# A two-layer hybrid decoder trunk on one core: first output projection on the right side of memory, last feed-forward sums in a region of their own, and another timing model for the order

## The chip, the cores and the metric

The kernel runs on one core of a Trainium2 chip. The metric is device time in microseconds; three runs of the kernel before gave 2640.45, 2644.82 and 2648.73, so the median is 2644.82 us.

## What is computed

The reference is a trunk of two layers over 1024 positions of width 1024, all in f32. Cut to what matters:

```python
for l in range(DEPTH):                                    # DEPTH = 2
    mod = cond @ w_mod[l] + b_mod[l]                      # 6 vectors of 1024
    sh1, sc1, gt1, sh2, sc2, gt2 = jnp.split(mod, 6)
    h = rms_norm(x, norm_g[l, 0]) * (1.0 + sc1) + sh1
    y = mixer_block(h, ...)     # h @ w_in, four mixers, group norms, @ w_o
    x = x + gt1 * rms_norm(y, norm_g[l, 1])
    h = rms_norm(x, norm_g[l, 2]) * (1.0 + sc2) + sh2
    y = jnp.square(jax.nn.relu(h @ w_up[l])) @ w_down[l]  # width 4096 inside
    x = x + gt2 * rms_norm(y, norm_g[l, 3])
```

The four mixers are a short gated convolution, sparse attention (compressed, selected and window branch, each a softmax), gated linear attention in chunks of 64, and a chunked gMLP.

## The kernel before

Activations stand with features on the 128 partitions, and 512 positions (one half, `hf`) are done at a time, so there are four rounds of mixer and feed-forward: `mix(0,0)`, `mix(0,1)`, `ff(0,0)`, `mix(1,0)`, `ff(0,1)`, `mix(1,1)`, `ff(1,0)`, `ff(1,1)`, written in that order in the code.

Each product is made of three matmuls (`mm3`, L173 to L175): weights and activations are split into a rounded high part and a rest, and high*high, high*low and low*high are summed in PSUM. So each weight tile of 128x512 that a DMA of 256 KB brings (`raw_a`, `raw_b` or `raw_f`, by lane) is cast by ACT (`A.copy(hi, raw)`, L167) and subtracted by DVE (`sub(lo, raw, hi)`, L131) before its twelve matmuls. The raw tiles have 3 buffers on lanes a and b, 5 on lane f.

The order of work on each engine is not written out by hand: the framework lists all instructions, simulates them with a timing model, and gives each engine a fixed queue, first come by priority. `tc.block(schedule_with_timeline_sim=True)` (L40 of the kernel) picks the model. Each engine then works strictly down its own queue on the chip. `LATER` (800 instructions) lowers the priority of the residual and norm after three of the four output projections.

What the steps of the change touch:

- `mods_start` and `load_x`: 16 rows of `w_mod` (`mw`, 512 KB each, 6 buffers) are multiplied with the condition on DVE (L239), and give the first scale and shift; `load_x(1)` brings the second half of x into the 8 tiles `y` that held the first half, so each of its loads waits until `make_h` has read the old tile.
- `mods_now(0, (2, 3, 4), "b")`: 48 tiles of `w_mod` through the 3 buffers `raw_b`, multiplied on DVE (L247), needed for the residual and norm that follow the first output projection. `mods_steps`: the other rows of `w_mod`, one step behind each `up` and behind every second `down` unit of `ff(0,0)` and `ff(0,1)`.
- The output projection (`gemm(p, "a", w_o[l, o], outs, ...)` in `mix`), its evacuations `yo` (L912), the sum of squares (`rms_R`, one matmul against ones at L195), `residual` (eight times L140 and L137, with `xo` loaded back from memory and the sum stored) and `make_h` (`nt`, `h`), which gives the feed-forward's input.
- `ff_body`: `up(n)` squares the ReLU (`r`, one buffer, then `hid`), `down(g)` adds eight units into the tiles `y` (L137), `finish` makes the residual of the feed-forward, with `xo` in the buffers of `hid`.
- Attention (`nsa_part`): scores (L786, L788) go to PSUM, DVE takes the maximum (L793, L799), ACT the exponential, DVE and ACT the scaling; `attend` transposes on PE (L741), splits into high and rest on ACT (L743) and DVE (L131), and multiplies with the values (L746, L747). Units of the feed-forward stand between these on PE's queue wherever the order puts them.

Of the kernel before, what the change touches and what calls it, by code (L numbers as in the profile page):

```python
# [7 lines left out]
F32 = mybir.dt.float32  # L8
# [8 lines left out]
DEPTH = 2  # L17
T = 512
# [17 lines left out]
def trunk_kernel(ctx, tc, xT, c, pos, freq, sel, w_in, conv_w, cmp_pos, cmp_w1, cmp_w2,  # L36
# [3 lines left out]
    ctx.enter_context(tc.block(schedule_with_timeline_sim=True))  # L40
# [253 lines left out]
    def mods_steps(todo):  # L294

        for l, j in todo:
            for k in range(8):
                mod_half(l, j, k, lambda src, shape: wraw("f", src, shape))
                if k == 7:
                    mod_scale(l, j, slice(0, 8))  # L300
                yield
# [574 lines left out]
    def mix(l, hf, h, between=None):  # L876
        d = par[l]
        gain = d["gain"]
        with ExitStack() as es:
            gr = es.enter_context(region("gates"))  # L880
            if l == 0 and hf == 0:
# [11 lines left out]
                lane_pool["f"] = pool("ff", side="right")  # L893
# [12 lines left out]
        with region("wo") as rg:  # L906
            y = []
            for o in range(8):
                p = ps("mm")
                gemm(p, "a", w_o[l, o], outs, range(8))  # L910
                yo = rg.tile([128, T], F32, name="yo", tag="yo", bufs=8)
                A.copy(yo, p)  # L912
                y.append(yo)
            if between is not None:
                res = between()
            with tc.high_priority(offset=-LATER[l, hf]):
                R = rms_R(y, 1.0 / 1024)
                residual(y, d["G1"], R,
                         lambda k: load(rg.tile([128, T], F32, name="xo", tag="xo", bufs=4),
                                        (xT[hf] if l == 0 else xb[hf])[:, k, :]), xa[l][hf])  # L920
                R = rms_R(y, 1.0 / 1024)
                h2[hf] = make_h(y, R, d["A2"], d["mod"][:, 3, :])
        return res

    def ff(l, hf, todo=()):
        if not todo:
            return ff_body(l, hf, None)
        steps = mods_steps(todo)
# [4 lines left out]
    def ff_body(l, hf, step):  # L933
# [28 lines left out]
        def down(g, cs=slice(0, T), ws=None):  # L962
            for n in range(8):
# [5 lines left out]
                if g == 0:  # L969
                    y[n] = ytile()  # L970
                    A.copy(y[n], p)
                else:
                    add(y[n][:, cs], y[n][:, cs], p)
# [11 lines left out]
        def finish(cs, R):  # L985
            residual(y, d["G2"], R,
                     (lambda k: xo[k]) if last else
                     (lambda k: load(ffp.tile([128, T], F32, name="xo", tag="hid", bufs=8), xa[l][hf][:, k, :])),
                     xb[hf] if l + 1 < DEPTH else out[hf], cs)
# [10 lines left out]
        for cs in parts:  # L1000
            down(NGRP - 1, cs, ws)
        Rs = [rms_R(y, 1.0 / 1024, cs=cs, mk=spare if last else nt) for cs in parts]
        for cs, R in zip(parts, Rs):
            finish(cs, R)
        return y
# [14 lines left out]
    xt = ff(0, 0, ((0, 5), (1, 1), (1, 0), (1, 2), (1, 4), (1, 3)))  # L1020
    h = norm(1, 0, xt)
    mix(1, 0, h)
    xt = ff(0, 1, ((1, 5),))
    h = norm(1, 1, xt)
# [90 lines left out]
```

## Time and profile before

| what | us |
|---|---|
| median of three runs | 2644.82 |
| the profiled execution, its own time | 2647.0 |
| its span, on which the shares below are taken | 2645.3 |
| PE (TensorE) busy | 2495.8 |
| DVE (VectorE) busy | 1629.1 |
| ACT (ScalarE) busy | 1308.1 |

The profile shows for each engine how long it worked, and for each wait of an engine which instruction of another engine, or which DMA, ended it. PEclk is the clock that was granted to TensorE as a share of 2.4 GHz. Matmuls overlap, so the time of one row is longer than its share of the engine's time; what one costs is read from a stretch with its count.

### The profile page before, as it was taken

The numbers are of one execution on the slowest core, as the hardware profiler recorded it, in microseconds if no ns is written. First come the engines' busy times: TensorE is split into PE (matmuls) and PEld (weight loads), VectorE is DVE, ScalarE is ACT, GpSimd is POOL, SyncE is SP. The second block draws the span as 40 slices with busy tenths as digits, with TensorE's granted clock in tenths as the row PEclk, the third lists the DMA queues.
The fourth block names the chain that finished last, engine by engine and source line by source line (L and its number), as shares of the span: only waits on it lengthen the run. The fifth ranks groups of instructions, "written<-read, shape, count | busy, mean of one in ns | idle before, by whom it ended". The sixth has DMA issues, their size and how long they took to land.

```text
span 2645.3 us, 34444 instructions
## 1 busy us (share of the span) xinstructions
PE 2495.8 (94%) x11834; PEld 1985.5 (75%) x11834; DVE 1629.1 (62%) x3425; ACT 1308.1 (49%) x2657; POOL 53.4 (2%) x65
## 2 busy tenths in 40 slices
PE   4899769999999998999999999999999999899997
PEld 2677447777788776877787877877788877688886
DVE  7576885466888468454576476544567846634445
ACT  4464444544566445444466445453466744444333
POOL 0100000000000000000100000000100000000000
PEclk9799889999999999999999999999999999999999
DMA  8212753345444346322322344222422133533332
GB/s 296 69 53 81 222 175 124 112 128 167 125 131 128 112 129 204 100 83 78 117 80 76 112 140 148 93 84 77 120 76 68 56 108 112 175 97 98 97 96 76
DMA packets 176200, 305.79 MB, mean 116 GB/s; under 512 B 21573, under 2 KB 33434, under 8 KB 176026
## 3 DMA queue, kind: packets, MB, share of 16 engines
q1 hardware_dynamic: 176026, 303.60, 37.1%
q8 instruction: 93, 1.52, 0.2%
q14 instruction: 81, 0.66, 0.1%
HBM read 281.50 MB, written 17.83 MB: 113 GB/s over the span
## 4 chain that ended last, share of the span: by engine, by line
PE 83%; DVE 8%; DMA 6%; issue 2%; ACT 1%; SPq 0%; POOL 0%; DVEq 0%; ACTq 0%; POOLq 0%
PE ps_ff L173 16%; PE ps_ff L174 16%; PE ps_ff L175 16%; PE ps_mm L173 7%; PE ps_mm L174 7%; PE ps_mm L175 7%; DMA raw_f<-in_w_mod_dram 1%; PE ps_pv L747 1%; PE ps_pv L746 1%; PE ps_mm L741 1%; DMA raw_b<-in_w_mod_dram 1%; PE ps_s L786 1%; PE ps_s L788 1%; PE ps_t L741 1%; PE ps_t L195 1%
## 5 line engine op out<-in xcount | busy, mean ns | idle before, releaser
L167 ACT CAST w_f<-raw_f 128x512 fp32r<-128x512 f32 x504 | 311.6, 619 | 462.9 <-PE ps_ff L174 432.5
L131 DVE TENSOR_TENSOR w_f<-raw_f,w_f 128x512 fp32r<-128x512 f32 x504 | 348.9, 693 | 222.8 <-ACT w_f L167 197.6
L173 PE MATMUL ps_ff<-h,w_f 128*128 128x512 f32 x1024 | 406.2, 397 | 30.8 <-ACT r L945 25.1
L175 PE MATMUL ps_ff<-h,w_f 128*128 128x512 f32 x1024 | 408.1, 399 | 0.0
L173 PE MATMUL ps_ff<-hid,w_f 128*128 128x512 f32 x992 | 394.3, 398 | 12.5 <-ACT nt L188 5.4
L174 PE MATMUL ps_ff<-h,w_f 128*128 128x512 f32 x1024 | 406.1, 397 | 0.0
L174 PE MATMUL ps_ff<-hid,w_f 128*128 128x512 f32 x992 | 391.5, 395 | 0.0
L175 PE MATMUL ps_ff<-hid,w_f 128*128 128x512 f32 x992 | 390.4, 394 | 0.0
L173 PE MATMUL ps_mm<-h,w_a 128*128 128x512 f32 x832 | 337.5, 406 | 12.6 <-ACT h L209 10.4
L175 PE MATMUL ps_mm<-h,w_a 128*128 128x512 f32 x832 | 336.7, 405 | 6.9 <-DVE w_a L131 6.7
L174 PE MATMUL ps_mm<-h,w_a 128*128 128x512 f32 x832 | 335.9, 404 | 7.4 <-DVE h L140 5.7
L167 ACT CAST w_a<-raw_a 128x512 fp32r<-128x512 f32 x208 | 128.8, 619 | 308.9 <-PE ps_mm L174 276.4
L131 DVE TENSOR_TENSOR w_a<-raw_a,w_a 128x512 fp32r<-128x512 f32 x208 | 143.1, 688 | 195.1 <-ACT w_a L167 174.9
L173 PEld LDWEIGHTS ps_ff<-h,w_f 128*128 128x128 f32 x1024 | 194.7, 190 | 77.5 <-ACT r L945 26.4
L137 DVE TENSOR_TENSOR y<-y,ps_ff 128x512 f32<-128x512 f32 (+1 forms) x232 | 154.2, 666 | 142.2 <-PE ps_ff L175 140.5
L173 PEld LDWEIGHTS ps_ff<-hid,w_f 128*128 128x128 f32 x992 | 187.0, 189 | 60.1 <-ACT nt L188 6.2
L175 PEld LDWEIGHTS ps_ff<-h,w_f 128*128 128x128 f32 x1024 | 194.6, 190 | 44.9 <-issue 4.1
L174 PEld LDWEIGHTS ps_ff<-h,w_f 128*128 128x128 f32 x1024 | 194.9, 190 | 42.7 <-issue 1.9
L175 PEld LDWEIGHTS ps_ff<-hid,w_f 128*128 128x128 f32 x992 | 186.9, 188 | 41.5 <-issue 1.9
L174 PEld LDWEIGHTS ps_ff<-hid,w_f 128*128 128x128 f32 x992 | 187.1, 189 | 41.3 <-issue 3.1
L173 PEld LDWEIGHTS ps_mm<-h,w_a 128*128 128x128 f32 x832 | 158.7, 191 | 60.2 <-ACT h L209 14.0
L174 PEld LDWEIGHTS ps_mm<-h,w_a 128*128 128x128 f32 x832 | 158.7, 191 | 50.5 <-DVE h L140 8.9
(363 smaller groups left out, 3494.5 us busy)
## 6 DMA issues: line engine op xcount, KB each, us to landing
raw_f<-in_w_up_dram SPq DMA_DIRECT2D x256, 256.0 KB, 2.8
raw_f<-in_w_down_dram SPq DMA_DIRECT2D x256, 256.0 KB, 2.6
raw_a<-in_w_in_dram SPq DMA_DIRECT2D x144, 256.0 KB, 2.7
raw_f<-in_w_mod_dram SPq DMA_DIRECT2D x112, 256.0 KB, 2.9
raw_a<-in_w_o_dram SPq DMA_DIRECT2D x64, 256.0 KB, 2.7
raw_b<-in_w_mod_dram SPq DMA_DIRECT2D x48, 256.0 KB, 3.3
mw<-in_w_mod_dram SPq DMA_DIRECT2D x16, 512.0 KB, 7.2
raw_b<-in_w_in_dram SPq DMA_DIRECT2D x32, 256.0 KB, 2.7
```

Source lines behind the costliest of these rows:

```text
L131: V.tensor_tensor(out=out, in0=a, in1=b, op=ALU.subtract)
L137: eng.tensor_tensor(out=out, in0=a, in1=b, op=ALU.add)
L167: A.copy(hi, raw)
L173: PE.matmul(ps_ap, wh, xh, start=start, stop=False)
L174: PE.matmul(ps_ap, wh, xl, start=False, stop=False)
L175: PE.matmul(ps_ap, wl, xh, start=False, stop=stop)
L195: PE.matmul(p, ones, acc, start=True, stop=True)
L741: PE.transpose(tp[0:kn, hh, :], cols(h0 + hh), ident)
L746: PE.matmul(pv[:, h0:h0 + nh, :], vst, th[0:kn], start=first[0], stop=False)
L747: PE.matmul(pv[:, h0:h0 + nh, :], vst, tl[0:kn], start=False, stop=last)
L786: PE.matmul(sp[:, 0:w], qh[:, h0 + hh, :], KX[:, 128 * k0:128 * k0 + w], start=True, stop=False)
L788: PE.matmul(sp[:, 0:w], ql[:, h0 + hh, :], KX[:, 128 * k0:128 * k0 + w], start=False, stop=True)
```

## The change

The order is now made with the framework's simpler timing model, as the line that picked the other one is gone. In the first mixer round only (`opening`), the region of the output projection stands on the right side of the on-chip memory, the eight inputs are taken in another order (attention and linear attention first), `xo` has 8 buffers in place of 4, and the feed-forward's pool is opened after that region and no longer before it. The steps of `mods_steps` begin after 5 calls in `ff(0,0)` and after 20 in `ff(0,1)`. For three of the four feed-forward rounds the last `down` group writes its sums into new tiles `yf` of a region `fin`, where also `xo` has its own 4 buffers, and the norm of the next layer is made in it; the last round, `ff(1,1)`, stays as it was.

```diff
-    ctx.enter_context(tc.block(schedule_with_timeline_sim=True))
...
-    def mods_steps(todo):
-
+    def mods_steps(todo, skip):
+
+        for _ in range(skip):
+            yield
...
-                lane_pool["f"] = pool("ff", side="right")
...
-        with region("wo") as rg:
+        opening = (l, hf) == (0, 0)
+        with region("wo", "right" if opening else "left") as rg:
...
-                gemm(p, "a", w_o[l, o], outs, range(8))
+                gemm(p, "a", w_o[l, o], outs, (6, 7, 4, 5, 2, 3, 0, 1) if opening else range(8))
...
-                         lambda k: load(rg.tile([128, T], F32, name="xo", tag="xo", bufs=4),
+                         lambda k: load(rg.tile([128, T], F32, name="xo", tag="xo", bufs=8 if opening else 4),
...
+        if opening:
+            lane_pool["f"] = pool("ff", side="right")
...
-        steps = mods_steps(todo)
+        steps = mods_steps(todo, 5 if hf == 0 else 20)
...
-                    add(y[n][:, cs], y[n][:, cs], p)
+                    yn = yo() if yo else y[n]
+                    add(yn[:, cs], y[n][:, cs], p)
+                    y[n] = yn
...
+        with region("fin") as rg:
+            down(NGRP - 1, yo=lambda: rg.tile([128, T], F32, name="yf", tag="yf", bufs=8))
+            R = rms_R(y, 1.0 / 1024)
+            finish(slice(0, T), R,
+                   lambda k: load(rg.tile([128, T], F32, name="xo", tag="xo", bufs=4), xa[l][hf][:, k, :]),
+                   xb[hf] if l + 1 < DEPTH else out[hf])
+            return norm(l + 1, hf, y) if l + 1 < DEPTH else None
```

No instruction of the computation is added or taken away; nearly all of them move. Three places show how. Lines of the kernel after are one less than before down to `mods_steps`, and one more behind the next few.

The first is the DMA queue (SP) at the program's start: `mw` are the first rows of `w_mod`, `y` the tiles of x (the first eight are the first half, the next eight the second), `raw_a` the first weights of the input projection. Before:

```order
L110 DMA conv_107<-in_conv_w_dram 128x6
L110 DMA gain_108<-in_gains_dram 128x8
L158 DMA raw_a<-in_w_in_dram 128x512 x2
L158 DMA raw_a<-in_cmp_w_dram 128x128
L265 DMA mw<-in_w_mod_dram 128x1024
L158 DMA raw_b<-in_w_in_dram 128x512 x3
L265 DMA mw<-in_w_mod_dram 128x1024 x4
L1011 DMA y<-in_xT_dram 128x512
```

And now:

```order
L264 DMA mw<-in_w_mod_dram 128x1024 x16
L109 DMA conv_97<-in_conv_w_dram 128x6
L109 DMA gain_98<-in_gains_dram 128x8
L109 DMA ng_104<-in_norm_g_dram 128x32
L109 DMA bmod_105<-in_b_mod_dram 128x48
L109 DMA conv_106<-in_conv_w_dram 128x6
L109 DMA gain_107<-in_gains_dram 128x8
L1022 DMA y<-in_xT_dram 128x512 x8
L157 DMA raw_a<-in_w_in_dram 128x512 x2
```

The first weights have moved behind all sixteen `mw` and behind the eight loads of the second half of x.

The second is DVE's queue where the residual of the output projection of `mix(0,1)` is made (`yo` with the factor `G`), while units of `ff(0,0)` run (`w_f`, `y`). Before:

```order
L137 TENSOR_TENSOR y<-y,ps_ff 128x512
L131 TENSOR_TENSOR w_f<-raw_f,w_f 128x512
L140 SCALAR_TENSOR_TENSOR yo<-yo,G_102,nt 128x512 x8
L137 TENSOR_TENSOR yo<-yo,xo 128x512
L137 TENSOR_TENSOR y<-y,ps_ff 128x512
L137 TENSOR_TENSOR yo<-yo,xo 128x512
L131 TENSOR_TENSOR w_f<-raw_f,w_f 128x512
L137 TENSOR_TENSOR yo<-yo,xo 128x512 x2
```

And now:

```order
L139 SCALAR_TENSOR_TENSOR yo<-yo,G_101,nt 128x512 x2
L130 TENSOR_TENSOR w_f<-raw_f,w_f 128x512
L136 TENSOR_TENSOR y<-y,ps_ff 128x512
L130 TENSOR_TENSOR w_f<-raw_f,w_f 128x512
L246 ISA raw_f,mp<-raw_f,cond 128x512
L246 ISA mp 128x1
L136 TENSOR_TENSOR yo<-yo,xo 128x512
L136 TENSOR_TENSOR y<-y,ps_ff 128x512
L130 TENSOR_TENSOR w_f<-raw_f,w_f 128x512
L139 SCALAR_TENSOR_TENSOR mod_108<-mp,bmod_105 128x1
L136 TENSOR_TENSOR yo<-yo,xo 128x512
L139 SCALAR_TENSOR_TENSOR yo<-yo,G_101,nt 128x512
```

The block of eight has become single instructions among those of the feed-forward, and steps of `mods_steps` (L246) have come between.

The third is PE's queue in the attention of `mix(0,1)`: `ps_s` are scores, `ps_t` and `ps_mm` from `bp` transposes, `ps_pv` the product with the values, `ps_ff` matmuls of the feed-forward. Before, where eighteen matmuls of the feed-forward follow one product of the values:

```order
L747 MATMUL ps_pv<-w_a,VS 128x512
L746 MATMUL ps_pv<-w_a,VS 128x512
L741 MATMUL ps_t<-ident,bp 128x128 x4
L173 MATMUL ps_ff<-h,w_f 128x512
L747 MATMUL ps_pv<-w_a,VS 128x512
L746 MATMUL ps_pv<-w_a,VS 128x512
L174 MATMUL ps_ff<-h,w_f 128x512
L175 MATMUL ps_ff<-h,w_f 128x512
```

And now:

```order
L172 MATMUL ps_ff<-hid,w_f 128x512
L787 MATMUL ps_s<-KW,qh 128x512
L789 MATMUL ps_s<-KW,ql 128x512
L747 MATMUL ps_pv<-w_a,VS 128x512
L808 MATMUL ps_s<-KW,qh 128x128
L809 MATMUL ps_s<-KW,ql 128x128
L808 MATMUL ps_s<-KW,qh 128x128
L748 MATMUL ps_pv<-w_a,VS 128x512
L747 MATMUL ps_pv<-w_a,VS 128x512
L742 MATMUL ps_mm<-ident,bp 128x128 x4
L809 MATMUL ps_s<-KW,ql 128x128
```

From the first score of an attention to the first matmul of its output projection there stood 729, 368 and 632 matmuls of the feed-forward in `mix(0,1)`, `mix(1,0)` and `mix(1,1)`; now there stand 267, 118 and 252. The others now follow the output projections, where the queue holds feed-forward alone for longer.

## Rows read from the trace of the kernel before

**Rows 1.** The page: span, PE and DVE in its first part, and the granted clock in forty slices.

```profile
span 2645.3 us, 34444 instructions
PE 2495.8 (94%) x11834; PEld 1985.5 (75%) x11834; DVE 1629.1 (62%) x3425; ACT 1308.1 (49%) x2657; POOL 53.4 (2%) x65
...
PEclk9799889999999999999999999999999999999999
```

**Rows 2.** Who PE waited for, over the whole span: us in total, times, longest us.

```profile
PE ps_t L195 <- DVE nt L137: 40.5, 3, 19.7
PE ps_ff L173 <- ACT r L945: 25.1, 3, 11.0
```

**Rows 3.** Busy time of each engine in stretches of 50 us: stretch and its length, PE, PEld, DVE, ACT, POOL with counts, granted clock, DMA share, GB/s.

```profile
350.00:400.00 50.00, 27.36 (x103) 20.29 (x102) 38.68 (x68) 22.07 (x36) 0.70 (x1) 0.76 0.43 141
...
950.00:1000.00 50.00, 44.12 (x183) 34.60 (x182) 41.92 (x69) 27.03 (x47) 0.00 (x0) 0.97 0.45 138
1000.00:1050.00 50.00, 40.23 (x165) 31.93 (x164) 41.13 (x84) 24.15 (x41) 0.76 (x1) 0.90 0.68 228
...
1500.00:1550.00 50.00, 44.70 (x190) 34.97 (x189) 33.73 (x54) 22.74 (x39) 0.00 (x0) 1.00 0.44 144
...
1600.00:1650.00 50.00, 45.00 (x183) 35.74 (x183) 35.86 (x56) 26.15 (x45) 0.00 (x0) 0.94 0.52 168
...
2200.00:2250.00 50.00, 46.97 (x195) 37.22 (x194) 34.96 (x55) 25.68 (x43) 0.00 (x0) 0.97 0.38 126
2250.00:2300.00 50.00, 39.00 (x163) 31.52 (x162) 36.30 (x58) 22.62 (x39) 0.00 (x0) 0.90 0.62 204
```

**Rows 4.** The same columns for the three attention stretches, from the first score to the output projection, and for 300 us of feed-forward alone.

```profile
621.50:867.40 245.90, 243.81 (x1180) 197.16 (x1178) 202.19 (x529) 152.98 (x371) 0.00 (x0) 1.00 0.43 132
1314.20:1435.70 121.50, 121.50 (x605) 98.86 (x602) 85.74 (x229) 81.89 (x213) 0.00 (x0) 1.00 0.27 78
1913.90:2133.20 219.30, 219.30 (x1084) 179.08 (x1084) 160.22 (x373) 145.49 (x353) 0.00 (x0) 1.00 0.24 69
2300.00:2600.00 300.00, 300.00 (x1325) 248.41 (x1324) 125.70 (x190) 122.21 (x205) 0.00 (x0) 1.00 0.33 100
```

**Rows 5.** DVE in order of time where `ff(1,0)` ends, and the matmul that waited: start, us, instruction, and in brackets the idle time before it and what ended it.

```profile
2280.10 5.38 DVE L140 SCALAR_TENSOR_TENSOR y<-y,G,nt 128x512 f32<-128x512 f32 x8
2285.40 1.29 DVE L137 TENSOR_TENSOR y<-y,xo 128x512 f32<-128x512 f32 x2
...
2290.82 0.68 DVE L131 TENSOR_TENSOR hid<-r,hid 128x512 fp32r<-128x512 f32 x1
...
2292.19 0.80 PE L173 MATMUL ps_ff<-h,w_f 128*128 128x512 f32 x1 [11.00 <-ACT r L945]
```

**Rows 6.** PE's instructions in order of time around 350 us (columns as in rows 5).

```profile
350.87 1.02 PE L195 MATMUL ps_t<-nt,ones 128*128 128x512 f32 x2
371.55 2.08 PE L195 MATMUL ps_t<-nt,ones 128*128 128x512 f32 x2 [19.66 <-DVE nt L137]
376.61 1.22 PE L173 MATMUL ps_ff<-h,w_f 128*128 128x512 f32 x2 [2.98 <-ACT h L209]
```

**Rows 7.** The 48 tiles of `w_mod` on lane b: the first 24 loads in the DMA queue in order of time, the last product on DVE, and the page's row of these loads (KB each, median us to landing).

```profile
254.95 34.38 SPq L158 DMA_DIRECT2D raw_b<-in_w_mod_dram  x24
...
334.50 0.68 DVE L247 CUSTOM_DVE_ANT_0 raw_b<-raw_b,cond 128x512 f32<-128x512 f32 x1
...
raw_b<-in_w_mod_dram SPq DMA_DIRECT2D x48, 256.0 KB, 3.3
```

**Rows 8.** The start: the first weights and the last load of x in the DMA queue, PE's first gemm matmul and the last of its first 48, DVE's groups of the first 54 us for lanes a and b, and stretches of 10 us (columns as in rows 3).

```profile
18.41 1.66 SPq L158 DMA_DIRECT2D raw_a<-in_w_in_dram  x2
...
49.70 0.33 SPq L1011 DMA_DIRECT2D y<-in_xT_dram  x1
...
29.40 0.80 PE L173 MATMUL ps_mm<-h,w_a 128*128 128x512 f32 x1 [0.80 <-ACT h L209]
...
52.62 0.40 PE L175 MATMUL ps_mm<-h,w_a 128*128 128x512 f32 x1
...
L131 DVE TENSOR_TENSOR w_a<-raw_a,w_a 128x512 fp32r<-128x512 f32 x5 | 3.4, 670 | 0.1
...
L131 DVE TENSOR_TENSOR w_b<-raw_b,w_b 128x512 fp32r<-128x512 f32 x2 | 1.4, 680 | 0.0
...
20.00:30.00 10.00, 4.26 (x7) 1.90 (x7) 9.56 (x20) 4.54 (x7) 0.00 (x0) 1.00 0.91 314
30.00:40.00 10.00, 3.21 (x6) 1.62 (x6) 9.81 (x21) 1.57 (x3) 0.00 (x0) 1.00 1.04 401
...
60.00:70.00 10.00, 7.99 (x28) 3.64 (x26) 2.13 (x5) 4.63 (x12) 0.00 (x0) 0.83 0.43 143
70.00:80.00 10.00, 8.87 (x26) 6.73 (x26) 5.80 (x11) 2.88 (x6) 2.56 (x2) 0.66 0.25 79
```

**Rows 9.** Groups of DVE's instructions in the whole span: count, busy us, mean ns of one, idle time before them and what ended it.

```profile
L131 DVE TENSOR_TENSOR w_f<-raw_f,w_f 128x512 fp32r<-128x512 f32 x504 | 348.9, 693 | 222.8 <-ACT w_f L167 197.6 <-PE ps_ff L175 20.1 <-PE ps_ff L174 2.6
L137 DVE TENSOR_TENSOR y<-y,ps_ff 128x512 f32<-128x512 f32 x216 | 147.6, 684 | 138.8 <-PE ps_ff L175 137.8
...
L131 DVE TENSOR_TENSOR hid<-r,hid 128x512 fp32r<-128x512 f32 x128 | 88.1, 688 | 62.4 <-ACT hid L948 62.1
...
L247 DVE CUSTOM_DVE_ANT_0 raw_f<-raw_f,cond 128x512 f32<-128x512 f32 x112 | 78.1, 699 | 65.1 <-DMA raw_f<-in_w_mod_dram 64.8
```

More of the change, by code (lines that the diff above doesn't have):

```diff
@@ L960, in wlast, with down @@
             return hi, lo
-        def down(g, cs=slice(0, T), ws=None):
+        def down(g, cs=slice(0, T), ws=None, yo=None):
             for n in range(8):
@@ L983, in ff_body, with finish @@
         xo = [load(spare(), xa[l][hf][:, k, :]) for k in range(8)] if last else None
[L985 to L989, printed above, removed]
+        def finish(cs, R, xo, o):
+            residual(y, d["G2"], R, xo, o, cs)
         for n in range(G):
@@ L999, in ff_body @@
         ws = [wlast(n) for n in range(8)] if last else None
[L1000 to L1005, printed above, removed]
+        if last:
+            for cs in parts:
+                down(NGRP - 1, cs, ws)
+            Rs = [rms_R(y, 1.0 / 1024, cs=cs, mk=spare) for cs in parts]
+            for cs, R in zip(parts, Rs):
+                finish(cs, R, lambda k: xo[k], out[hf])
+            return None
+        with region("fin") as rg:
[5 more added lines that the diff above has]
+            return norm(l + 1, hf, y) if l + 1 < DEPTH else None
     def load_x(hf):
@@ L1019, in trunk_kernel @@
     mix(0, 1, h)
-    xt = ff(0, 0, ((0, 5), (1, 1), (1, 0), (1, 2), (1, 4), (1, 3)))
-    h = norm(1, 0, xt)
+    h = ff(0, 0, ((0, 5), (1, 1), (1, 0), (1, 2), (1, 4), (1, 3)))
     mix(1, 0, h)
-    xt = ff(0, 1, ((1, 5),))
-    h = norm(1, 1, xt)
+    h = ff(0, 1, ((1, 5),))
     mix(1, 1, h)
```

## Prediction

> **What bounds the kernel now.** Read the page first: PE is busy for 2495.8 of 2645.3 us, DVE for 1629.1 [rows 1]. PE's work is the same before and after, so a change of order can only touch the 149.5 us in which PE stands idle and the stretches in which it runs at a lower clock. Then read who PE waits for: two waits hold 65.6 us, the sum of squares (L195) behind DVE's additions, 40.5 us, and the first matmul of a feed-forward unit behind ACT's `r`, 25.1 us [rows 2]. Both are the same thing, a residual and norm of some sixteen 0.6 to 0.7 us instructions that DVE does in one block while PE's queue needs something behind it. Then read where: the stretches of 50 us show it at 350, at 950 to 1050, at 1500, at 1600 and at 2200 to 2300, and in all but one of them the granted clock falls too [rows 3]. Last read what is well filled: in the three attention stretches PE is idle for 2.1 of 586.7 us, though DVE works 82%, 71% and 73% of them [rows 4]. One matmul of feed-forward alone costs 300.00 / 1325 = 0.2264 us [rows 4]; that is the unit of all that follows.
>
> The sum is made against the profiled execution's own 2647.0 us (its span of 2645.3 and 1.7 around it); the median of the three runs is 2.2 lower, and so is the forecast.
>
> **The later boundaries: -35 us.** The stretches from 950 to 1050, 1500, 1600 and 2200 to 2300 hold 5.9 + 9.8 + 5.3 + 5.0 + 3.0 + 11.0 = 40.0 us of idle PE, and their granted clocks of 0.97, 0.90, 0.94, 0.97 and 0.90 cost 1.3 + 4.0 + 2.7 + 1.4 + 3.9 = 13.3 more: 53 us [rows 3]. After an output projection the residual no longer stands as a block but between the feed-forward units, which are there in plenty because the attention used fewer; DVE has time for them, since in feed-forward alone it is busy for 125.7 of 300 us [rows 4]. I leave 2 us there. At the end of a feed-forward the block does not go. In `ff(1,0)` the subtraction `hid` for which PE waits began 10.7 us after the residual's first instruction [rows 5]. In the order of the change it stands behind 8 scalings (5.4 us), 6 additions (3.7 us) and, but for `ff(1,0)`, two sums (1.3 us), while PE has 31 matmuls (7.0 us) from where the block begins: 3.4 us of wait, and by the ratio of the 1600 stretch (2.7 of clock to 5.0 of idle) 2 us of clock. Three such ends make 16, so 18 of 53 stay. Own `xo` buffers in `fin` let these loads start without `hid`'s buffers; with 4 of them the fifth load waits for the first addition, and four further vector instructions stand before its use. I give that nothing. Bounds: -45, if the waits go wholly, and -15, if the blocks only change places.
>
> **The first output projection: -4 us.** At 350 the wait of 19.66 us ends with a sum of squares at 371.55, and the feed-forward starts at 376.61 [rows 6]; 22.6 us idle and a clock of 0.76 over 27.4 us of work make 29 us lost [rows 3]. PE's queue had this sum of squares and the feed-forward before the rest of the next mixer; now the mixer's matmuls come first, so this wait goes. But the 48 tiles of `w_mod` come earlier in DVE's queue: all of their products now stand before the weights of the fourth of eight output tiles. In the trace they took from 254.95 to 335.2, 80 us [rows 7]. In front of PE are then 31 matmuls of the convolution and 72 of the projection, 23 us. From the first of these loads to 376.61 PE did some 276 matmuls of gemms in 121.7 us. Now, at the trace's pace, 80 us and then the other 173 in 39 us make 119; at the pace that three buffers allow (3.3 us to landing, 0.69 for the product, 0.33 for the issue, through three: 1.44 us a tile [rows 7]) 69 + 39 = 108. A residual block in front of the next mixer's weights costs 10 us of DVE against 26 matmuls, 6 us: 4 more. Between -10 and +2; I take the middle. The other order of inputs lets the projection begin before the convolution's part is split; that lies behind the same DVE queue and is costed at nothing. The right side and the later pool only decide which memory the loads wait for; 8 `xo` in place of 4 end the waits inside the residual, which the mixer's matmuls now cover. Bounds for all this: -12 and +8.
>
> **The start: +5 us.** The first weights of the input projection now wait behind eight loads of x, each of which waits for DVE to have read the old tile. In the trace DVE is busy for 9.6 and 9.8 of 10 us there, the weights were issued at 18.41, the last of those eight loads at 49.70, and PE began at 29.40 and had 48 matmuls done at 53.0 [rows 8]. Without the five `w_a` and two `w_b` subtractions (4.8 us) DVE comes to that read about 46; issue, landing and cast put PE's first gemm near 50, and 48 matmuls take 10.9 us and 2 more at the lower clock: 63 instead of 53. Some 5 come back between 60 and 80, where PE lost 3.1 us of idleness and, at clocks of 0.83 and 0.66, 4.4 us [rows 8], since the rope matmuls now stand among gemms. Bounds: -3 and +12. The first attention, with its linear attention and gMLP, is mixed anew as well; no row separates it, so 0, with 10 us each way, a tenth of a hundred us, which is what the clock of 0.7 to 0.9 there leaves open [rows 1].
>
> **The three later attentions: +17 us.** With 462, 250 and 380 matmuls fewer, their stretches would be 245.9 - 104.6 = 141, 121.5 - 56.6 = 65 and 219.3 - 86.0 = 133 us of PE, 339 in all, if PE stayed as full. DVE loses 41, 19 and 30 weight subtractions, 40 products of `w_mod` (the first stretch alone), 28, 13 and 24 additions of `y`, 7, 7 and 9 of `hid`, at 693, 699, 684 and 688 ns [rows 9]: 80, 27 and 43 us, which leaves 122, 59 and 117. That is 86%, 91% and 88% of PE's time, where it was 82%, 71% and 73%. Behind a product with the values there is less on PE's queue that waits for nobody, and a score, its softmax and the split must come round through ACT and DVE. The nearest row is the stretch with 82%, which lost 1%; the far one is 950 to 1050, where PE waited on vector blocks and lost 21 of 100 us with the clock [rows 3]. I take 5%, 17 us, near the nearest; ends 0 and 68. The matmuls taken out run later at 0.2264 each, where nothing else is needed. The shift of `mods_steps` by 5 and 20 calls moves 0.7 us products into units in which DVE is half idle: nothing.
>
> The sum: -35 - 4 + 5 + 17 = -17, so 2630 against 2647.0, and **2628** against the median.
>
> The Trainium skill ("TensorE: Matmul & The Clock Gate", section "HAM oscillation — how this bites in real kernels") says that an array which falls idle between bursts, again and again, is put back to its slower clock each time, so that every burst begins slow. The trace agrees at the blocks, where idle time and a granted clock of 0.76 to 0.97 come together [rows 3]; in the attention the clock is 1.00, with PE full [rows 4].
>
> **The rivals.** *The attention starves PE (slower).* If the three stretches lose 20%, as at 950 to 1050, they cost 68 and not 17: 2679. For it: DVE at 86 to 91%, ACT close behind, and chains through three queues in fixed order. Against it: the first stretch at 82% lost 1%. It decides from a tenth on: 34 us use up the gain.
> *The clock falls there too.* Short waits that recur bring the lower clock: at 0.83, as at 60 to 70 us [rows 8], 339 us cost 70 more: 2698. For it: every idle stretch of rows 3 but one. Against it: waits under a microsecond did not do it in rows 4. This is what the skill's rule above would make of it.
> *The blocks only change places.* If half of the 35 stays, because residual and norm hold up another unit, the time is 2646, no change. For it: the end of a feed-forward still has its block. Against it: eight scalings in a row are gone after the projections.
> *The attention costs nothing.* Then 2611. For it: the 82% stretch. Against it: 91% has no precedent in this trace.
>
> **Chances.** A difference under 0.3% (8 us) cannot be told from none. Forecast 0.42, with 2612 to 2642 as its own range; attention free 0.12; blocks change places 0.16; attention starves 0.22; clock too 0.08. Faster is the forecast but a tenth, and the free attention: 0.50. Same is most of the changed places and the rest of the forecast: 0.18. Slower is 0.32. The range runs from 2595, somewhat under the free attention, to 2685, somewhat over the starved one.
>
> **What would show it.** The wait of the sum of squares behind DVE falls from 40.5 to under 15 us; the feed-forward's wait for `r` to about 10, with three ends of 3 to 4. The attention stretches last about 148, 68 and 140 us, at a clock of 1.00, with DVE over 80%. PE's first gemm starts near 50 us. In the fourth tile of the first projection PE waits 30 us or more for a weight subtraction, and none of 20 us for a sum of squares follows. I am wrong if PE is idle for more than a tenth of the attention, if the clock falls there, or if the blocks at the feed-forward's ends cost as much as before.

## The result, and the profile after

The changed kernel takes 2674.64 us (median of 4 runs, 2670.19 to 2678.22) where the kernel before takes 2643.7 on the same chip: a ratio of 1.0112, interval 1.01 to 1.0125. It is 31 us slower; 2628 had been forecast, and the time lies in the upper part of the range that went to 2685. The profiled execution of after has a span of 2668.5 us, 23.2 more than that of before [rows 1]; that is less than 31 because it is the shortest of the four (2670.19), while that of before, at 2647.0, is longer than its median. What follows accounts for the 23.

The page of after: span, busy time, and of the 40 slices the rows of PE and of its granted clock.

```profile
span 2668.5 us, 34592 instructions
...
PE 2503.8 (94%) x11834; PEld 1971.2 (74%) x11834; DVE 1635.8 (61%) x3425; ACT 1315.0 (49%) x2657; POOL 52.6 (2%) x65
...
PE   2999489999999998999999998999999999999998
...
PEclk9999699999999999999999999999999999999999
```

PE's row shows two holes, the first slice (2 tenths) and the fifth (4 tenths, with a clock of 0.6); the fifth is the first output projection. Who PE waited for (us in total, times, longest):

```profile
PE ps_mm L172 <- ACT w_a L166: 37.6, 3, 31.2
PE ps_t L194 <- DVE nt L136: 31.0, 6, 16.8
PE ps_ff L174 <- DVE w_f L130: 19.5, 3, 8.2
PE ps_mm L172 <- ACT yo L913: 16.1, 1, 16.1
```

The wait of a unit of feed-forward for ACT's `r`, 25.1 us [rows 2], is gone. In its place stands one of 19.5 us for `w_f` behind DVE, three times (8.2, 7.0 and 4.3), which no step of the prediction names. The 31.2 us of the first row are the start of the program, the first gemm. Of the 31.0 for the sum of squares, 16.8 are at the start too, where before had 16.2.

Stretches of 50 us (width, then busy us and count of PE, of the weight loads, DVE, ACT and POOL, the granted clock, DMA share, GB/s):

```profile
0.00:50.00 50.00, 2.08 (x2) 0.50 (x2) 39.44 (x88) 18.14 (x28) 1.51 (x9) 1.00 0.81 277
...
250.00:300.00 50.00, 31.19 (x119) 22.98 (x118) 37.66 (x94) 17.15 (x30) 0.00 (x0) 0.80 0.52 164
300.00:350.00 50.00, 28.06 (x102) 20.56 (x101) 39.66 (x99) 18.30 (x30) 1.16 (x1) 0.76 0.64 207
...
750.00:800.00 50.00, 47.30 (x199) 37.89 (x198) 46.11 (x95) 24.09 (x41) 0.00 (x0) 0.97 0.68 215
...
1000.00:1050.00 50.00, 42.48 (x183) 33.77 (x182) 33.31 (x53) 24.17 (x41) 0.00 (x0) 0.96 0.39 129
1050.00:1100.00 50.00, 49.23 (x197) 37.86 (x198) 32.54 (x55) 22.24 (x38) 0.64 (x1) 0.94 0.34 103
...
1650.00:1700.00 50.00, 42.87 (x173) 32.81 (x172) 39.25 (x63) 26.59 (x45) 0.81 (x1) 0.93 0.44 139
...
1850.00:1900.00 50.00, 49.80 (x255) 38.05 (x254) 41.77 (x120) 40.71 (x116) 0.00 (x0) 1.00 0.14 41
...
2300.00:2350.00 50.00, 45.72 (x192) 36.92 (x192) 23.86 (x36) 21.77 (x38) 0.00 (x0) 0.97 0.46 147
```

Beside [rows 3] and [rows 4]: the stretches that hold the end of a feed-forward (1000 to 1100, 1650, 2300) still lose idle time and clock; the one at 1850 lies in the third of the later attentions and is full. The stretch at 300 is the first output projection.

Where the 23 us came from is read at equal places in PE's queue: the same instruction of before and after, and each feed-forward matmul that stands in a stretch more or fewer counted at the 0.2264 us of [rows 4]. The times are those of the instructions in the two traces, the counts those of all of PE's matmuls between them; they differ by feed-forward matmuls alone.

| stretch | before: us, matmuls | after: us, matmuls | after minus before, counts evened out | forecast |
|---|---|---|---|---|
| start to the gMLP of mixer (0,1) | 419.3, 1558 | 412.9, 1478 | +11.7 | +1 |
| rest of mixer (0,1), to the last gemm of the attention's inputs | 185.6, 917 | 122.2, 619 | +4.1 | 0 |
| mixer (1,0) from its convolution, to the same gemm | 242.1, 1160 | 162.2, 787 | +4.5 | 0 |
| mixer (1,1), likewise | 241.5, 1158 | 162.2, 787 | +4.7 | 0 |
| three later attentions, to the output projection | 262.6, 135.8, 229.7 (1279, 767, 1173) | 152.1, 81.2, 148.1 (798, 499, 784) | -1.6, +6.1, +6.5 | +17 |
| projection (0,1) to convolution (1,0) | 190.4, 730 | 371.6, 1514 | +3.7 | in the -35 |
| projection (1,0) to convolution (1,1) | 226.2, 915 | 371.5, 1568 | -2.5 | in the -35 |
| projection (1,1) to the last feed-forward matmul | 498.8, 2174 | 671.8, 2997 | -13.3 | in the -35 |

The sum is +23.9. The attentions cost 11, the boundaries give back only 12, the opening costs 12, and the mixers 13.

In the mixers the loss is in part plain idle time. Mixer (1,0), before and then after, in the columns of the stretches above:

```profile
1057.90:1300.00 242.10, 242.10 (x1162) 191.85 (x1161) 122.81 (x224) 106.75 (x198) 9.28 (x11) 1.00 0.30 91
```

```profile
1058.80:1221.00 162.20, 159.34 (x789) 120.83 (x788) 89.92 (x175) 73.69 (x142) 10.26 (x12) 1.00 0.27 85
```

With 411 feed-forward matmuls among its own, PE never stood; with 38 it stands for 2.9 of the 4.5 us.

### The profile page after: what moved, and what is told of

Same layout as the page of the kernel before. It is cut to its first block, busy times and chain, and to the rows that moved or that the text cites. A ratio compares the mean times of both kernels' runs of the same rounds, so it can differ in the third digit from the quotient of the medians.

```text
span 2668.5 us, 34592 instructions
## 1 busy us (share of the span) xinstructions
PE 2503.8 (94%) x11834; PEld 1971.2 (74%) x11834; DVE 1635.8 (61%) x3425; ACT 1315.0 (49%) x2657; POOL 52.6 (2%) x65
## 5 line engine op out<-in xcount | busy, mean ns | idle before, releaser
L174 PE MATMUL ps_ff<-h,w_f 128*128 128x512 f32 x1024 | 405.6, 396 | 19.5 <-DVE w_f L130 19.5
L136 DVE TENSOR_TENSOR y<-y,ps_ff 128x512 f32<-128x512 f32 (+1 forms) x208 | 138.3, 665 | 173.9 <-PE ps_ff L174 172.6
```

What stands on the lines that cost most here:

```text
L136: eng.tensor_tensor(out=out, in0=a, in1=b, op=ALU.add)
L174: PE.matmul(ps_ap, wl, xh, start=False, stop=stop)
```

## The experiments

All twelve are compared with the kernel before on the same chip; its medians there lie between 2644.5 and 2647.4 us (2643.7 beside the changed kernel), so differences of a few microseconds between two of these runs say nothing. First, which part of the change costs the time.

**All edits, the old model.**

```diff
+    ctx.enter_context(tc.block(schedule_with_timeline_sim=True))
```

> The kernel after, with the old timing model put back; regions, the opening and the skipped steps stay as changed. Theory A (the model's order costs the 31 us): about 2645, within 10 of the kernel before. Theory B (the regions, the opening and the skipped steps cost them, whatever the model): 2665 to 2680. If the edits help under the old model too, it falls under 2636.

2646.28 us, ratio 0.9999 (0.999 to 1.0009): theory A.

**The model alone.** The kernel before without that line, and no other edit.

```diff
-    ctx.enter_context(tc.block(schedule_with_timeline_sim=True))
```

> The kernel before, with the one line of the timing model taken out and nothing else. Theory A: 2675 or more (more, if the other edits were made to mend this order: then 2685 to 2720). Theory B: about 2645.

2668.1 us, ratio 1.0084 (1.006 to 1.0108), between the two theories and nearer to A. So the timing model by which the order is made costs about 22 us by itself; the edits cost nothing under the old model, and under the new one some 6, which is not clear of the noise (the changed kernel's interval begins at 1.01). Counted as in the table, the trace of this run loses 2.3 us in the opening, 14.3 in the mixers and 11.8 in the attentions, and gains 8.8 at the boundaries: the losses of mixers and attentions come with the model alone, most of the opening's only where model and edits meet (the edits under the old model lose 2.9 there). That the edits as a whole are neutral does not mean that each is; two stretches of the run with all edits and the old model point to one that pays:

```profile
950.00:1000.00 50.00, 49.67 (x216) 40.19 (x216) 40.01 (x64) 28.90 (x49) 0.00 (x0) 1.00 0.53 175
1000.00:1050.00 50.00, 49.59 (x216) 40.00 (x215) 36.49 (x58) 30.35 (x51) 0.00 (x0) 1.00 0.50 160
```

The kernel before lost 5.9 and 9.8 us of idle time here, with a clock of 0.97 and 0.90 [rows 3].

**The second half's x later.**

```diff
-    xt = load_x(1)
+    with tc.high_priority(offset=-400):
+        xt = load_x(1)
```

> The kernel after, with the loads of x's second half put later in the DMA queue, behind the first weights. If the first weights' place behind these loads costs the opening its time, PE's first gemm moves from 50 to about 30 to 40 us and the time falls by 5 to 10 us against the kernel after (2665 to 2670). If the opening is held by DVE's products of w_mod anyway, under 3 us.

2672.91 us, ratio 1.0103 (1.0084 to 1.0122). PE's first gemm starts at 43.3 instead of 50.0, not at 30 to 40, and the whole gains under 2 us, less than can be told from nothing: what is won at the start is not found again at the end.

**The opening's edits undone.**

```diff
-        opening = (l, hf) == (0, 0)
+        opening = False
...
+                lane_pool["f"] = pool("ff", side="right")
```

> The kernel after, with the first output projection on the left again, inputs in the old order, 4 buffers for xo and the pool opened before it. If this part helps the new order, the time rises to 2680 to 2700. If the wait of 31 us in the projection's fourth tile comes from it, the time falls to 2650 to 2660 and that wait goes; if it comes from the 48 tiles of w_mod in front, the wait stays and the time is within 5 us of 2675.

2675.97 us, ratio 1.0118 (1.0101 to 1.0136): no difference in the whole. The wait of 31 us that the expectation puts into the projection's fourth tile is the one at the start of the program; in the projection the wait of 16.1 us for `yo` is gone, and behind it one of 16.9 for the sum of squares stands again, as in the kernel before (19.7). In its trace the gMLP of mixer (0,1) is reached at 409.7 us, with the counts evened out as early as before, so the 11.7 us of the opening are gone there; by the convolution of (1,0) it stands at +18.4, where the changed kernel has +17.9. The opening's edits move a loss of 12 us in front of that gMLP; without them it falls behind it, in the rest of mixer (0,1) (+6.3 in place of +4.1), in its attention (+3.0 in place of -1.6) and after its projection (+9.1 in place of +3.7). Why was not found.

**The modulation steps at their old place.**

```diff
-        steps = mods_steps(todo, 5 if hf == 0 else 20)
+        steps = mods_steps(todo, 0)
```

> The changed kernel with the modulation steps at the first feed-forward units again (no calls skipped). Theory A (the 4 us that ff(0,0) loses beside these steps come with the steps wherever they stand): 2675, within 4. Rival (the moved steps are what helps ff(0,0) against the kernel with the model alone, whose stretch 750 to 850 lost 13 us where the changed kernel lost 5): 2680 to 2686. Second rival (the move costs): 2668 or less.

2676.41 us, ratio 1.0131 (1.0112 to 1.0149). The skip is worth nothing in the whole that can be told here, as forecast and as theory A says.

Second, what in the new order costs it. The table says that the mixers lost their filler, the feed-forward units that stood among their matmuls, and take some 13 us longer.

**Filler back by priority, 60 and 200 steps.**

```diff
-    mix(0, 1, h)
+    with tc.high_priority(offset=-60):
+        mix(0, 1, h)
```

(and `mix(1, 0, h)`, `mix(1, 1, h)` likewise; the other run has -200.)

> The changed kernel, with the mixers of (0,1), (1,0) and (1,1) put back by 60 steps of priority, so that feed-forward units again stand among their matmuls: in PE's queue some 310 to 320 between the convolution and the last projection of the attention's inputs, and about 420 in the attention, where the changed kernel has none and 130 to 270. Theory A (what the simpler timing model costs is the missing filler: about 13 us in the three mixers and 11 in the attentions, while the gain at the boundaries stays): 2674 - 24 = 2650, range 2640 to 2658. Theory B (the new order inside the stages costs the time, on DVE, ACT or the DMA queues, and filler does not help): 2668 to 2680.

> As the run with 60 steps, with 200: 100 to 180 feed-forward matmuls more in the mixers and attentions, and 53 (12 us) of the next feed-forward between the end of one and the next convolution. Theory A (filler, and cover at the ends of the feed-forwards, where the changed kernel loses 13 + 10 us at the first two): 10 us less than with 60 steps, 2640, range 2628 to 2652; the waits of the matmul with the ones fall from 31 us to under 15. Theory B (filler does not help): 2668 to 2680. Rival C (the feed-forward's units run out before the residual after the output projection is done, as in the kernel before, and that wait comes back): 2655 to 2670, with a wait for ACT r or a sum of squares of over 10 us.

2834.86 us (ratio 1.0721, 1.0705 to 1.0737) and 2850.34 us (1.0778, 1.0762 to 1.0794). All theories missed this by over 150 us. The 60 steps also put more there than the expectation says: some 630 to 670 feed-forward matmuls more in each mixer, not 310 to 320, and 438 to 694 in the attentions, not about 420. Waits and stretches of the run with 60 steps:

```profile
PE ps_t L194 <- DVE nt L136: 82.3, 8, 17.7
...
PE ps_ff L172 <- DVE yf L136: 36.4, 3, 12.2
```

```profile
1000.00:1050.00 50.00, 25.51 (x100) 18.56 (x99) 27.62 (x42) 19.50 (x34) 0.00 (x0) 0.75 0.43 137
...
1700.00:1750.00 50.00, 20.72 (x73) 15.08 (x72) 37.02 (x56) 20.20 (x32) 0.00 (x0) 0.69 0.34 111
```

The sum of squares is waited for 82.3 us, and stretches after the projections are down to 25.51 and 20.72 us of PE at clocks of 0.75 and 0.69. At equal places in PE's queue the three stretches from an output projection to the end of the feed-forward behind it cost about 73 us more than before (changed kernel: 12 fewer), the attentions 51 (11 more), the mixers 52 (13 more). The first number is rival C of the second run, far beyond its size: a unit that is spent as filler is missing behind the projection. The others are no want of filler. In mixer (1,1) PE's queue now changes 910 times within 1447 matmuls between feed-forward and mixer, 104 times within 1158 in the kernel before. From one start to the next it takes 259 ns in the mean where a feed-forward matmul is followed by one of the mixer (242 in the kernel before), and 217 the other way (208 before), so a pair of changes takes 26 ns more, which over 455 pairs is 12 of the 18 us that this mixer loses. In this order, filler one matmul at a time costs more than none. That the changing itself is the cause is argued: no run has as much filler in larger pieces, and at the 104 changes of before other matmuls stand.

**Filler back in blocks.** The feed-forward is made a generator, and one unit of it is written behind each gemm of the gates, the linear attention and the attention's inputs.

```diff
+    def fill():
+        if unit.get(0) is not None:
+            next(unit[0])
...
         gemm(p, lane, w_in[l, GLA0], h)
+        fill()
...
-        steps = mods_steps(todo, 5 if hf == 0 else 20)
+        steps = mods_steps(todo, 14 if hf == 0 else 29)
```

(The modulation steps so begin nine calls later; what that is worth by itself was not run.)

> The changed kernel with the next feed-forward written out unit by unit behind the gemms of the gates, the linear attention and the attention's inputs, so that 178, 85 and 85 of its matmuls stand there in blocks of 12 and 24, where the changed kernel has none; in the attention nearly the same number stays. Theory A (the run with 60 steps failed because its filler came one matmul at a time and in such number that none was left for the blocks after the projections; the 4.4 us that each mixer loses beside the kernel before are for want of filler): 8 to 13 us less, 2664, range 2658 to 2669. Theory B (filler in the mixers costs as much as it covers, so its want explains nothing): 2671 to 2680. Theory C (as with 60 steps, each such matmul makes it worse): over 2685.

2667.01 us, ratio 1.008 (1.006 to 1.01). Theory A, inside its range: 7.6 us less at the median, just short of the 8 to 13, though the two intervals touch and the profiled span is only 3.2 shorter (its opening, which the edit does not touch, took 3.7 longer). In the table's terms mixers (1,0) and (1,1) lose 2.9 and 3.1 us instead of 4.5 and 4.7, with 123 feed-forward matmuls in each instead of 38; mixer (0,1) loses 4.4, no less, though it has 192 instead of 14. The idle time of mixer (1,0) is about halved:

```profile
1062.80:1242.60 179.80, 178.25 (x873) 137.05 (x874) 95.11 (x183) 82.03 (x157) 10.11 (x12) 1.00 0.28 88
```

So filler in blocks pays in two of the three mixers, a third of what its want was held to cost there, and a fifth over all three. That is little: in the traces of runs that leave these two mixers alone they lose between 3.4 and 4.7. Theory C, that any filler does harm, falls.

**The next feed-forward put forward by 300 steps.**

```diff
-    h = ff(0, 1, ((1, 5),))
+    with tc.high_priority(offset=300):
+        h = ff(0, 1, ((1, 5),))
```

(and the other two.)

> The changed kernel with the three feed-forwards ff(0,0), ff(0,1) and ff(1,0) put forward by 300 steps of priority. In PE's queue that changes little but the end of ff(0,0), where 197 matmuls of ff(0,1) instead of 72 now stand before the next convolution, and the end of ff(1,0); the mixers and attentions keep their order. Theory A (the ends of the feed-forwards cost 13, 10 and 6 us in the changed kernel because too little that waits for nobody stands behind them): 8 us come back at the first, 2 or 3 at the third: 2664, range 2658 to 2670, and the wait of the matmul with the ones falls from 31 us to under 20. Theory B (the end waits on the vector block itself, whatever stands behind it in the queue): 2671 to 2678.

2659.38 us, ratio 1.005 (1.0034 to 1.0066): about 15 us less, within theory A's range and half as much again as its 10 or 11. The sign that it named failed: the wait for the matmul with the ones is 34.9 us, not under 20. The three ends, the first in two stretches as it lies later here:

```profile
1000.00:1050.00 50.00, 49.67 (x217) 39.88 (x216) 25.06 (x39) 24.31 (x41) 0.00 (x0) 1.00 0.31 95
1050.00:1100.00 50.00, 48.19 (x205) 37.50 (x204) 39.64 (x65) 30.59 (x53) 0.85 (x1) 1.00 0.48 152
...
1650.00:1700.00 50.00, 43.09 (x172) 32.95 (x171) 35.13 (x57) 23.25 (x39) 0.64 (x1) 0.90 0.41 132
...
2300.00:2350.00 50.00, 49.70 (x219) 40.84 (x218) 17.49 (x27) 24.55 (x43) 0.00 (x0) 1.00 0.34 100
```

The first and the third are mended (42.48 at 0.96 with 49.23 at 0.94, and 45.72 at 0.97, in the changed kernel), the second is not: there PE still waits 6.8 us for `w_f`. At the third the residual has left: it is made at 2529 to 2546, in the midst of ff(1,1), and there too single weights stand among it. At the first it is what stands in DVE's queue that differs. DVE at the end of ff(0,0) in this run (start, duration):

```profile
1055.12 1.42 DVE L139 SCALAR_TENSOR_TENSOR yf<-yf,G,nt 128x512 f32<-128x512 f32 x2 [2.04 <-ACT nt L199]
1056.45 0.68 DVE L130 TENSOR_TENSOR w_f<-raw_f,w_f 128x512 fp32r<-128x512 f32 x1
1057.05 1.28 DVE L136 TENSOR_TENSOR yf<-yf,xo 128x512 f32<-128x512 f32 x2
...
1059.52 0.68 DVE L130 TENSOR_TENSOR w_f<-raw_f,w_f 128x512 fp32r<-128x512 f32 x1
```

A weight of the next feed-forward (`w_f`) comes after every two or three instructions of the residual. In the changed kernel's own trace it does not:

```profile
1034.72 0.69 DVE L130 TENSOR_TENSOR w_f<-raw_f,w_f 128x512 fp32r<-128x512 f32 x1 [2.51 <-ACT w_f L166]
1035.33 1.41 DVE L139 SCALAR_TENSOR_TENSOR yf<-yf,G,nt 128x512 f32<-128x512 f32 x2
...
1047.55 0.68 DVE L130 TENSOR_TENSOR hid<-r,hid 128x512 fp32r<-128x512 f32 x1
...
1049.35 0.68 DVE L136 TENSOR_TENSOR nt<-nt 128x512 f32<-128x512 f32 x1
1049.95 0.68 DVE L130 TENSOR_TENSOR w_f<-raw_f,w_f 128x512 fp32r<-128x512 f32 x1
```

The residual begins at 1035.33, and the weight half that PE needs is subtracted only at 1049.95, 14.6 us later. PE, in the same place:

```profile
1050.69 0.80 PE L174 MATMUL ps_ff<-h,w_f 128*128 128x512 f32 x1 [8.18 <-DVE w_f L130]
```

**Both together.**

```diff
         g, unit[0] = unit[0], None
-        return rest(g)
+        with tc.high_priority(offset=300):
+            return rest(g)
```

> The changed kernel with both: the next feed-forward written out unit by unit in the three mixers, and what is left of it put forward by 300 steps. In PE's queue 192 matmuls now stand between the end of ff(0,0) and the next convolution, and 185 at the end of ff(0,1), where the changed kernel has 72 and 72 and the run with 300 steps alone 197 and 72; the mixers keep their units. Theory A (the ends lack cover and the mixers lack filler, and there are units enough for both): the 15 us of the run with 300 steps, 4 to 8 of the run with units, and 7 more at the end of ff(0,1): 2674 - 28 = 2646, range 2640 to 2653; the stretch of 50 us that holds the end of ff(0,1) shows PE at 48 us or more. Theory B (both live on the same units, which then lack elsewhere): 2656 to 2665.

2665.97 us, ratio 1.0071 (1.0054 to 1.0088): slower than the run with 300 steps alone, as theory B says, if a microsecond beyond its range. The edit did not do what the expectation says: mixers (1,0) and (1,1) have not kept their units but hold 38 and 36 feed-forward matmuls, as in the changed kernel. The units are spent at the ends, and there the wait for `w_f` still stands, 7.5 and 4.6 us (8.2 and 7.0 in the changed kernel):

```profile
PE ps_ff L174 <- DVE w_f L130: 12.2, 2, 7.5
```

This is so although 213 feed-forward matmuls now start between the last addition into `yf` of ff(0,0) and the next convolution, where the changed kernel has 69 and the run with 300 steps 146. DVE there:

```profile
1081.96 0.69 DVE L130 TENSOR_TENSOR hid<-r,hid 128x512 fp32r<-128x512 f32 x1 [0.98 <-ACT hid L967]
1082.57 1.41 DVE L139 SCALAR_TENSOR_TENSOR yf<-yf,G,nt 128x512 f32<-128x512 f32 x2
...
1095.53 0.68 DVE L136 TENSOR_TENSOR nt<-nt 128x512 f32<-128x512 f32 x1
1096.13 0.68 DVE L130 TENSOR_TENSOR w_f<-raw_f,w_f 128x512 fp32r<-128x512 f32 x1
```

The residual comes later, at 1082.57, and is a block again: 13.6 us to the next `w_f`, and PE has by then used up its weights. Of the 213 matmuls 48 are left when the residual begins, as in the changed kernel (49); the run with 300 steps has 99 left. So more matmuls in front of the block only put the stall off. Where weights stand among the residual's instructions, it is gone, and there more matmuls are left behind the residual's start as well; as these need those weights, no run parts the two.

Last, a version that beats both kernels.

**The old model with only the region for the last sums.** Of the edits only `fin` is kept: `down` adds its last group into `yf`, and `norm` follows there.

```diff
+        with region("fin") as rg:
+            down(NGRP - 1, yo=lambda: rg.tile([128, T], F32, name="yf", tag="yf", bufs=8))
```

> The kernel before, with its timing model, and of the edits only the own region for the last feed-forward sums. By the trace of the run with all edits under the old model, the ends of ff(0,0) and ff(0,1) then lose 26 us less, the end of ff(1,0) 8 more, and what was lost there in the opening and after the moved modulation steps (17 us at 550 to 700 and 1250 to 1350) is absent here. Theory A (edits and model are separate, this one is a gain that the others hid): 2647 - 18 = 2629, range 2618 to 2640. Rival (a gain at one boundary is given back at the next, whatever else is done): 2643 to 2649.

2631.54 us, ratio 0.9952 (0.9937 to 0.9967), as theory A said in the whole. In its parts it was too large: counted as in the table, the trace gains 7 and 13 us where ff(0,0) and ff(0,1) end and loses 4 behind, where 26 less and 8 more were expected. Beside [rows 3] (40.23 at 0.90 and 45.00 at 0.94):

```profile
1000.00:1050.00 50.00, 47.38 (x204) 37.89 (x204) 42.81 (x87) 27.88 (x48) 0.00 (x0) 1.00 0.64 212
...
1600.00:1650.00 50.00, 49.58 (x215) 39.67 (x214) 36.89 (x58) 30.59 (x53) 0.00 (x0) 1.00 0.48 153
```

**The same in layer 0 alone.** ff(1,0) keeps its old end.

```diff
-        if last:
+        if l + 1 == DEPTH:
```

> As the run with the old model and the region for the last sums, but with the old end for ff(1,0), so that only ff(0,0) and ff(0,1) add into the region. In that run the end of ff(1,0) cost 17 us more than before, of which 12 came back in ff(1,1). Theory A (the region helps where a norm and a mixer follow, and costs 5 us net where only ff(1,1) follows): 2626, range 2621 to 2630. Rival (the end's place in the order moves with what precedes it, and nothing is saved): 2630 to 2636.

2633.21 us, ratio 0.9953 (0.9937 to 0.9969): the same. The end of ff(1,0) comes 14 us earlier in the trace (2245.0 against 2259.1), and nothing of it is left at the last feed-forward matmul (2617.8 against 2615.4). The rival is right.

## Why the prediction was wrong, point by point

**The start, +5: right in kind and size.** PE's first gemm starts at 50.0 us, as forecast, and up to the convolution of (0,0) the loss is 7.3 us, within -3 to +12.

**The first output projection, -4: within its bounds, by another wait.** The 48 products of `w_mod` ran from the first issue at 262.6 to 333.4, 71 us, between the 69 and 80 of the working, and the 20 us for a sum of squares [rows 6] are gone. But PE stood 4.69 us for the ones and then 16.06 not for a weight subtraction, as forecast (30 or more), but for a copy of a finished output tile by ACT. And the other order of the inputs, costed at nothing, was not free: the attention's part, now the first, was not yet split when PE came to it, and PE waited 7.97 us (3.3 in the run with the opening's edits undone). PE there:

```profile
292.23 0.79 PE L172 MATMUL ps_mm<-h,w_a 128*128 128x512 f32 x1 [7.97 <-ACT h L221]
...
312.31 2.07 PE L194 MATMUL ps_t<-nt,ones 128*128 128x512 f32 x2 [4.69 <-DVE nt L136]
330.44 0.79 PE L172 MATMUL ps_mm<-h,w_a 128*128 128x512 f32 x1 [16.06 <-ACT yo L913]
331.03 0.63 PE L173 MATMUL ps_mm<-h,w_a 128*128 128x512 f32 x1
331.46 0.63 PE L174 MATMUL ps_mm<-h,w_a 128*128 128x512 f32 x1
...
335.67 0.39 PE L172 MATMUL ps_mm<-h,w_a 128*128 128x512 f32 x1
335.90 0.39 PE L173 MATMUL ps_mm<-h,w_a 128*128 128x512 f32 x1
```

and ACT:

```profile
329.19 0.72 ACT L208 ACTIVATE h<-nt,mod 128x512 fp32r<-128x512 f32 x1 [0.62 <-DVE nt L139]
329.82 1.05 ACT L913 COPY yo<-ps_mm 128x512 f32<-128x512 f32 x2
```

The copy stood in ACT's queue behind the casts of the next norm, which wait for DVE's scalings, which stand among the products of `w_mod`. I had followed DVE's queue and PE's, not ACT's. The projection came to +4.4 in place of -4. The same rows show what such a wait costs behind it: the next starts are 0.43 us apart, and 0.23 from 335.67 on. These are the two levels of 1.2 and 2.4 GHz, and the stretch has a granted clock of 0.76. The Trainium skill ("TensorE: Matmul & The Clock Gate", section "HAM oscillation — how this bites in real kernels") says that an array idle between bursts begins the next one slow; the trace agrees.

**The mixers, 0: the step that was missing.** The 0 for "the first attention, with its linear attention and gMLP" was weighed for the first mixer; for the later ones I counted what DVE gains when filler goes, for the attentions alone, and never what PE loses in the gates, the linear attention and the attention's inputs. They lose 4.1, 4.5 and 4.7 us. That idle time comes where the filler goes is shown, and that filler in blocks gives some 1.6 us back in each of two mixers; that want of filler is all of it is not. In the run with all edits and the old model mixers (0,1) and (1,0) lose 6.8 and 4.2 us with 325 and 411 feed-forward matmuls, where the kernel before has 312 and 411, so something else can cost as much there.

**The attentions, +17: right, a little high.** They cost -1.6, +6.1 and +6.5, at a clock of 1.00 and DVE over 80% (41.77 of 50 us at 1850). The first of them is no dearer though it lost 481 matmuls of filler. The loss hardly shows as idle time: PE is busy 49.80 of 50 us. It is in the matmuls themselves. The product of a lower half of weights with the values, in the third attention, before and then after (count, busy us, mean ns, idle):

```profile
L747 PE MATMUL ps_pv<-w_a,VS 128*128 128x512 f32 x26 | 10.6, 408 | 0.0
```

```profile
L748 PE MATMUL ps_pv<-w_a,VS 128*128 128x512 f32 x26 | 12.3, 473 | 0.2
```

The mean rises from 408 to 473 ns, and from its start to the start of the next matmul in the queue from 246 to 335, which over 26 is 2.3 of the 6.5 us; the rest is spread over the other forms. So a PE that is full at full clock can still be slow; that what is added is waiting for operands is argued, not shown.

**The boundaries, -35: wrong, the largest miss.** They gave 12. By the sum of idle time and clock of the stretches, 53 us before, 18 were to stay. After the projections I left 2; there stay 10, of which 8.4 are between 750 and 950 (50 - 47.30 x 0.97 = 4.1 in the first stretch), where the products of `w_mod` and the residual fill DVE for 46.11 of 50 us. That these are the cause is argued: in the run with the steps at their old place the same stretches lose 13.6, in one trace, and the whole shows no change. At the ends I left 16; there stay 9.2 + 3.7 at 1000 to 1100, 10.1 at 1650 and 5.7 at 2300, each 50 - busy x clock: 29. The step that failed is "3.4 us of wait". It took `hid` as what PE waits for behind 8 scalings, 6 additions and two sums. `hid` came 12.2 us after the residual's first instruction, not far from the 10.4 worked out; but the next unit's weight stood behind it, at 14.6, with waits of 8.2, 7.0 and 4.3 in place of three of 3.4. The queue was right and the instruction in it wrong. One reading was wrong as well: of the 40.5 us for the sum of squares [rows 2], which I took for residual and norm, 16.2 are PE's first instruction at the start and 4.6 a sum of squares at 276.26, so the sign "under 15 us" could hardly be met; of the 24.3 behind the start 14.2 stay.

**The skipped steps, 0: right**, under the new model.

**The rivals.** "Blocks only change places", held at 0.16, comes nearest: of the 35 us at the boundaries 23 stayed away, at the ends of the feed-forwards by just that mechanism. "The attention starves PE" did not happen, nor did the clock fall in the attention. No rival put a loss in the mixers or the opening. -17 was the sum, and the terms missed it by +10.7 (opening), +13.3 (mixers), -6 (attentions) and +22.9 (boundaries): the boundaries alone undo the gain, and mixers and opening make it a loss. That the time lies within the range is luck: its upper end stood for a starved attention.

What stays open: why the loss of the opening, once undone, comes back from mixer (0,1) on; how much of the attentions' 11 us is for want of filler, since no way was found to put whole units there; and the four fifths of the mixers' loss that blocks of filler did not give back.

## What to carry to other kernels

When a change gathers work that had been spread as filler, price every stage that the filler leaves, PE's side as well as the vector engine's, and not only those where its arrival helps. Where a block of vector work stands at a boundary, list what its queue holds for the *next* unit, weights above all, and spread that among the block: where weights stood between the residual's instructions the stall was gone, and some 140 more matmuls in front of the block left it as it was. Follow every engine's queue past the block, the one that empties PSUM too.

## What the runs showed that was not expected

- Filler in single matmuls, 698 of them in mixer (1,1) where the kernel before has 409 and the changed kernel 38, made the kernel 160 us slower than hardly any; 85 to 178 more in blocks of 12 and 24 made it up to 8 us faster. The two differ in number as well as in grouping.
- A PE that is busy for 49.80 of 50 us at a clock of 1.00 lost some 4% of the third attention (6.5 of 148.1 us); it was read from equal places in the queue, and a third of it from the starts behind one form of matmul, not from idle time.
- One edit, the region for the last sums, is a gain of 0.5% under the old model, which the rest of the edits hid there.
